# Tables of a state-space layer: the rotation table stays in SBUF, tiles share the operand ring, six table buffers, and the table build gets the last rank

## The chip, the cores and the metric

The kernel runs on one core of one Trainium2 chip. The metric is the device time of one execution in microseconds (us), as the median of several executions. Differences of under 0.3%, 8 us, are about what a measurement of this kernel cannot tell from no change.

## What is computed

Two layers on x, 1024 tokens by 1024 channels in float32. Layer 0 mixes tokens with RWKV-7, layer 1 with a diagonal complex state-space layer (S5) behind which stands a gated linear unit (GLU). A dense MLP with squared ReLU follows each mixer, and after each of the four sublayers comes `LayerNorm(alpha * x + f(x))`. The mixer of layer 1, cut:

```python
def s5_mix(x, a_re, a_im, log_dt, b_re, b_im, c_re, c_im, d_skip, w_glu):
    mag = exp(dt * lam_re)                       # 64 groups x 64 states
    abar = mag * (cos(dt * lam_im) + i sin(dt * lam_im))
    bbar = (abar - 1) / lam * b                  # per group: 64 states x 16 channels
    # state over 1024 tokens, per group: h[t] = abar * h[t-1] + bbar @ u[t]
    y = real(c @ h) + u * d_skip
    z = gelu(y) @ w_glu
    return z[..., :d] * sigmoid(z[..., d:])

def sq_relu_mlp(x, w1, w2):
    return square(relu(x @ w1)) @ w2
```

## The kernel before

**Layout.** Channels lie on partitions. The tokens go in two halves of 512, A (`hA`, split operands `oAh`, `oAl`) and B (`hB`, `oBh`, `oBl`); each half is eight tiles of 128 x 512. Large products are made of three matmuls on operands that are split into a high and a low part (`mm3`): `whi` by the high part of x, `whi` by the low one, `wlo` by the high one. The products go to PSUM tiles `d`.

**Weights.** `wload` brings one 128 x 512 weight tile: a load on SP's DMA queue into `wraw` (two buffers), a cast to `whi` on ScalarE (ACT), a subtraction that gives `wlo` on VectorE (DVE). `whi` and `wlo` have three buffers each. SP issues nearly all transfers of the program, in program order; an issue that must wait for a buffer or for its data holds all that stand behind it.

**Order.** A scheduler orders each engine's instructions by a simulated timeline and by a priority number, lower first. The main line counts from 200000; `with rank(n)` gives a block of code other numbers. Before, the tables have 99500 (`S5R`), the layer norms 99000, `s5(0)` 99300 and `s5(1)` 99400, so all of these go ahead of the MLPs' work when they are ready.

**The main line around the change.** MLP of layer 0 on half A (`ma`) begins; the RWKV's output projection `wo(1)` for half B follows, sixteen weight tiles `wraw<-in_wo_dram`; then the rest of `ma`. Beside these `s5_tables()` builds the tables. Then `s5(0)` on half A stands beside the MLP of layer 0 on half B (`mb`), and `s5(1)` on half B beside the GLU of half A.

**The tables.** `s5_tables()` first makes the powers of abar, `pw`, from small 128 x 32 tiles (traced as `q`, numbered). `turns()` raises the angle to the eighth power and then doubles up a table `R` of 64 rotations (cosine, sine) and a third plane with the decay `mag`; it writes `R` to DRAM as `tR`, eight writes of 390 KB. Then, for each of eight blocks `f`, DVE expands `ca` and `bp` (lines 1261 to 1268), TensorE multiplies and transposes them, and ACT writes a padded tile `kpad`, from which eight small DMAs make a Toeplitz table `tT`; `tB` and `tC` are written also. These go to DRAM.

**The SSM.** `s5(H, h)` handles a half in four pairs of blocks. `inputs(f2)` transposes two tiles of h (`pu1` to `u1`), regroups them (`pu2` to `ug`), loads the block's `rot` from `tR` and `tb` from `tB`, and multiplies (`pbu`). `states` rotates the result, runs a scan with the decay (`tensor_tensor_scan`, twice for each block) and rotates back into `hb`. `outputs(f2)` loads `tt` and `tcm`, accumulates `py` from the inputs and the states, copies it to `y1`, transposes (`pyt`), makes `yg` with the skip and the GELU, and stores it to `s_y`. `yload` reads `s_y` back and splits it for the GLU. `tb`, `tt` and `tcm` share the tag `tab` with four buffers of 512 KB; `u1` and `y1` share a tag with two. `optile(H)` hands out the next tile of the ring that holds the split operands of half H.

The decay scan reads the third plane of the loaded table, whose first column is zero for each of its four groups:

```python
V.tensor_tensor_scan(gf, rot[:, 2].rearrange("p g n -> p (g n)"), gf, 0.0, op0=ALU.mult, op1=ALU.add)
```

Of the kernel before, what the change touches and what calls it, by code (L numbers as in the profile page):

```python
# [29 lines left out]
S5R = 99500  # L30
# [3 lines left out]
JB = 4  # L34
LN8R = 400000
# [37 lines left out]
def trunk(ctx, tc, A):  # L73
# [1046 lines left out]
    tR = dr.tile([KT, 128, 3, 4, NSC + 1], F32, name="tR")  # L1120

    def turns(rp, mg, re, im, x, y):

        R = rp.tile([128, 3, 32, NSC + 1], F32, name="R")
        V.memset(R[:, :, :, 0], 0.0)
        for _ in range(SL.bit_length() - 1):
            V.tensor_mul(x, re, re)
            V.tensor_mul(y, im, im)
            V.tensor_mul(im, re, im)
            V.tensor_sub(re, x, y)  # L1130
            V.tensor_scalar(im, im, 2.0, None, op0=ALU.mult)
            V.tensor_mul(mg, mg, mg)
# [9 lines left out]
        V.tensor_copy(R[:, 0, :, 1], re)  # L1142
        V.tensor_copy(R[:, 1, :, 1], im)
        unit(R[:, 0, :, 1], R[:, 1, :, 1])
        S.copy(R[:, 2, :, 1:], mg.unsqueeze(2).broadcast_to([128, 32, NSC]))
        j = 1
        while j < NSC:
            sp_ = [128, 2, 32, j]
            w1, w2 = (rp.tile([128, 2, 32, NSC // 2], F32, tag=nm, name=nm, bufs=1)[:, :, :, 0:j] for nm in ("rx", "ry"))
            a, b = R[:, 0:2, :, 1 : j + 1], R[:, 0:2, :, j + 1 : 2 * j + 1]  # L1150
            V.tensor_mul(w1, a, R[:, 0:1, :, j : j + 1].broadcast_to(sp_))
            V.tensor_mul(w2, a, R[:, 1:2, :, j : j + 1].broadcast_to(sp_))
            V.tensor_sub(b[:, 0], w1[:, 0], w2[:, 1])
            V.tensor_add(b[:, 1], w1[:, 1], w2[:, 0])
            j *= 2
            unit(R[:, 0, :, j], R[:, 1, :, j])
        for f in range(KT):
            SP.dma_start(tR[f], R[:, :, 4 * f : 4 * f + 4])

    def s5_tables():  # L1160
# [40 lines left out]
        V.tensor_mul(pw[:, 1, :, 1], mg, tq)  # L1201
        for j in (1, 2, 4):

            sp_ = [128, 2, 32, j]
            w1, w2 = (pp.tile([128, 2, 32, 4], F32, tag=nm, name=nm, bufs=1)[:, :, :, 0:j] for nm in ("wx", "wy"))
# [26 lines left out]
        kpads = [pq.tile([128, 4, 16, 16], F32, name=f"kpad{j}") for j in range(2)]  # L1232
# [3 lines left out]
        bc = pq.tile([128, 2, 2, 32, 16], F32, name="bc")  # L1236
# [3 lines left out]
        bb, b2, c2 = (pq.tile([128, 2, 32, 16], F32, name=nm) for nm in ("bb", "b2", "c2"))  # L1240
# [7 lines left out]
        S.copy(b2[:, 1], bb[:, 0])  # L1248
        for ri in range(2):
            S.mul(c2[:, ri], bc[:, 1, 1 - ri], -1.0)  # L1250
        c1 = bc[:, 1]
        S.mul(c1[:, 1], c1[:, 1], -1.0)
        for f in range(KT):
# [3 lines left out]
            ca = pq.tile([128, 4, 2, 9, 16], F32, tag="ca", name="ca", bufs=1)  # L1257
            bp = pq.tile([128, 4, 2, 8, 16], F32, tag="bp", name="bp", bufs=1)

            def expand(dst, x, y, npow):  # L1260
                S.copy(dst[:, :, :, 0], x[:, :, gs].rearrange("p r g c -> p g r c"))
                w = pq.tile([128, 4, 2, 8, 16], F32, tag="tw", name="tw", bufs=1)[:, :, :, 0 : npow - 1]
# [27 lines left out]
            bs = pq.tile([128, 4, 2, 128], F32, tag="bs", name="bs", bufs=1)  # L1290
# [7 lines left out]
        late.close()  # L1298

    def s5(H, h):  # L1300
        ug, hs = [], []

        def inputs(f2):

            u1 = s5p.tile([128, 2, 8, 4, 16], F32, tag="u1", name="u1", bufs=2)
            for j in range(2):
# [4 lines left out]
                S.copy(u1[:, j].rearrange("p g s c -> p s g c"), p.rearrange("p s (g c) -> p s g c", g=8))  # L1311
            for j in range(2):
                f = 2 * f2 + j
                p = pc.tile([128, HT], F32, tag="c", name="pu2").rearrange("p (g n) -> p g n", g=8)
                for g in range(8):
                    for e in range(2):
                        PE.matmul(p[64 * (1 - e) : 64 * (1 - e) + 64, g], u1[:, j, g].rearrange("p s c -> p (s c)"),  # L1317
                                  sel[:, e], start=True, stop=True)
# [13 lines left out]
                states(f, p, rot)  # L1332

        def states(f, p, rot):
# [4 lines left out]
            def temps():  # L1339
                return [optile(H, l).bitcast(F32).rearrange("p (r g n) -> p r g n", r=2, g=4) for l in "hl"]  # L1340

            g = s5p.tile([128, 2, 4, NSC + 1], F32, tag="g", name="g", bufs=2)
            h_ = s5p.tile([128, 2, 4, NSC + 1], F32, tag="hb", name="hb", bufs=4)
            for t in (g, h_):
                if H == 0:
                    V.memset(t[:, :, :, 0], 0.0)
                else:
                    V.tensor_copy(t[:, :, :, 0], cy[:, :, 4 * f : 4 * f + 4])
            t1, t2 = temps()
# [7 lines left out]
            t1, t2 = temps()  # L1357
            V.tensor_mul(t1, g[:, :, :, 1:], cos)
            V.tensor_mul(t2, g[:, :, :, 1:], sin)
            V.tensor_sub(h_[:, 0, :, 1:], t1[:, 0], t2[:, 1])  # L1360
            V.tensor_add(h_[:, 1, :, 1:], t1[:, 1], t2[:, 0])
            if H == 0:
                V.tensor_copy(cy[:, :, 4 * f : 4 * f + 4], h_[:, :, :, NSC])
# [229 lines left out]
```

## Time and profile before

| | us |
|---|---|
| median of three executions | 2673.59 (2672.07 to 2679.01) |
| the profiled execution | 2674.25 |
| its span | 2672.5 |
| PE busy | 2495.2 (93%) |
| DVE busy | 1846.4 (69%) |
| ACT busy | 1133.2 (42%) |
| POOL busy | 629.8 (24%) |
| mean granted clock of TensorE | 0.96 |

The median is over three executions without a profile; the durations come from the profiled one, whose span runs from its first instruction to its last. PE is TensorE's matmuls, PEld its weight loads, DVE is VectorE, ACT is ScalarE, POOL is GpSimd, SP issues DMAs. A row of a wait reads: waiting engine, operation and line, the releaser, then total us, times, longest us. Matmuls are pipelined, so their busy time overlaps. A granted clock of 0.50 means that TensorE ran at half speed. In names such as `wraw_11913<-in_wo_dram` the number tells buffers apart, and the left side is written from the right one.

### The profile page before, as it was taken

Reading aid. Unit: us, or ns where it says so; the run is one execution under the profiler, and the core shown is the slowest. Engines: PE = TensorE matmul, PEld = TensorE weight load, DVE = VectorE, ACT = ScalarE, POOL = GpSimd, SP = SyncE. Lnnn points to the kernel's source line nnn. Section 1 sums busy time; section 2 is a strip of 40 time slices with the busy share of each in tenths; the row PEclk is TensorE's granted clock in tenths of the full one; section 3 lists DMA queues with packets and bytes.
Section 4 is the critical chain, followed back from the end, with each engine's and each line's share of the span. In section 5 each row is a group of like instructions: output and inputs, shape, how many; then the busy total and the mean of one; then the engine's idle time right before and its main releaser. Section 6 shows DMA issues by size and latency. Waiting matters only on the chain.

```text
span 2672.5 us, 43745 instructions
## 1 busy us (share of the span) xinstructions
PE 2495.2 (93%) x16624; PEld 2022.1 (76%) x16624; DVE 1846.4 (69%) x3271; ACT 1133.2 (42%) x2028; POOL 629.8 (24%) x532
## 2 busy tenths in 40 slices
PE   7899979989889999888899999998999999999996
PEld 5678757788667777766777888886777888888875
DVE  7367677487896868799785555775587656565576
ACT  7555665554444334245433333433453322323234
POOL 3121542342442222011100011200233313223111
PEclk9999889998889999999999999998999999999998
DMA  4765455663323324456465333264222111111133
GB/s 152 243 217 182 155 166 178 206 183 126 97 74 92 93 93 141 132 155 154 148 224 179 99 95 96 90 210 143 91 83 79 56 51 52 52 51 52 52 103 99
DMA packets 213074, 330.31 MB, mean 124 GB/s; under 512 B 20736, under 2 KB 85376, under 8 KB 212864
## 3 DMA queue, kind: packets, MB, share of 16 engines
q1 hardware_dynamic: 212864, 327.52, 39.3%
q8 instruction: 131, 2.15, 0.3%
q14 instruction: 79, 0.65, 0.1%
HBM read 260.28 MB, written 67.16 MB: 123 GB/s over the span
## 4 chain that ended last, share of the span: by engine, by line
PE 54%; DVE 11%; DMA 4%; issue 2%; ACT 1%; SPq 1%; POOL 1%; ACTq 0%; DVEq 0%; POOLq 0%
PE d L198 40%; PE d L1040 9%; DVE wlo L153 2%; DMA wraw<-in_mw_dram 2%; DMA yl<-s_y 1%; PE pu L1317 1%; DVE hA L1003 1%; PE pbu L1331 1%; DVE qbuf L153 0%; DVE hA L880 0%; ACT whi L152 0%; PE py L1383 0%; DMA s_y<-yg 0%; DVE tw L1267 0%; DVE ca L1266 0%
## 5 line engine op out<-in xcount | busy, mean ns | idle before, releaser
L152 ACT CAST whi<-wraw 128x512 fp32r<-128x512 f32 x524 | 324.3, 619 | 748.5 <-PE d L198 430.3
L153 DVE TENSOR_TENSOR wlo<-wraw,whi 128x512 fp32r<-128x512 f32 x524 | 409.1, 782 | 271.9 <-ACT whi L152 266.0
L198 PE MATMUL d<-qbuf,whi 128*128 128x512 f32 (+1 forms) x1344 | 414.5, 391 | 21.4 <-DVE hA L1003 13.7
L198 PE MATMUL d<-oAh,whi 128*128 128x512 f32 (+1 forms) x768 | 310.8, 412 | 14.2 <-ACT ev L428 9.3
L198 PE MATMUL d<-oAh,wlo 128*128 128x512 f32 (+1 forms) x768 | 309.4, 409 | 9.7 <-DVE wlo L153 6.3
L198 PE MATMUL d<-oAl,whi 128*128 128x512 f32 (+1 forms) x768 | 306.7, 403 | 8.2 <-DVE oAl L153 8.2
L198 PEld LDWEIGHTS d<-qbuf,whi 128*128 128x128 f32 x1344 | 248.5, 192 | 80.2 <-DVE hA L1003 15.8
L198 PE MATMUL d<-qbuf,wlo 128*128 128x512 f32 (+1 forms) x672 | 259.3, 388 | 6.5 <-DVE wlo L153 6.3
L987 POOL TENSOR_TENSOR rl<-rl 128x512 f32<-128x512 f32 x80 | 90.8, 1136 | 704.2 <-ACT rl L986 677.9
L198 PE MATMUL d<-oBh,whi 128*128 128x512 f32 x512 | 204.0, 400 | 13.5 <-ACT whi L152 10.4
L198 PE MATMUL d<-oBh,wlo 128*128 128x512 f32 x512 | 203.7, 399 | 8.1 <-DVE wlo L153 8.1
L198 PE MATMUL d<-oBl,whi 128*128 128x512 f32 x512 | 202.5, 396 | 0.0
L198 PEld LDWEIGHTS d<-oAh,whi 128*128 128x128 f32 (+1 forms) x768 | 147.3, 194 | 49.2 <-ACT ev L428 11.6
L198 PEld LDWEIGHTS d<-oAh,wlo 128*128 128x128 f32 (+1 forms) x768 | 147.2, 193 | 44.9 <-DVE wlo L153 8.5
L198 PEld LDWEIGHTS d<-oAl,whi 128*128 128x128 f32 (+1 forms) x768 | 147.8, 194 | 39.3 <-DVE oAl L153 10.1
L198 PEld LDWEIGHTS d<-qbuf,wlo 128*128 128x128 f32 x672 | 128.1, 191 | 35.0 <-DVE wlo L153 9.4
L198 PE MATMUL d<-qh,wlo 128*128 128x512 f32 x384 | 151.4, 394 | 0.0
L198 PE MATMUL d<-ql,whi 128*128 128x512 f32 x384 | 150.6, 392 | 0.0
L198 PE MATMUL d<-qh,whi 128*128 128x512 f32 x384 | 149.3, 389 | 0.0
L198 PEld LDWEIGHTS d<-oBh,whi 128*128 128x128 f32 x512 | 97.3, 191 | 37.8 <-ACT whi L152 12.4
L1003 DVE TENSOR_TENSOR hB<-hB,d 128x512 f32<-128x512 f32 (+1 forms) x168 | 104.4, 632 | 30.6 <-PE d L198 28.8
L198 PEld LDWEIGHTS d<-oBh,wlo 128*128 128x128 f32 x512 | 97.4, 190 | 31.7 <-DVE wlo L153 10.0
(455 smaller groups left out, 5175.1 us busy)
## 6 DMA issues: line engine op xcount, KB each, us to landing
wraw<-in_mw_dram SPq DMA_DIRECT2D x376, 256.0 KB, 2.7
wraw<-in_glu_dram SPq DMA_DIRECT2D x64, 256.0 KB, 2.7
low<-wlo SPq DMA_DIRECT2D x52, 256.0 KB, 2.8
wlo<-low SPq DMA_DIRECT2D x52, 256.0 KB, 3.8
raw<-in_mw_dram SPq DMA_DIRECT2D x48, 256.0 KB, 2.6
wraw<-in_wk_dram SPq DMA_DIRECT2D x32, 256.0 KB, 3.4
wraw<-in_wr_dram SPq DMA_DIRECT2D x32, 256.0 KB, 4.0
wraw<-in_wv_dram SPq DMA_DIRECT2D x32, 256.0 KB, 4.4
```

Source lines behind the costliest of these rows:

```text
L152: S.copy(hi, src)
L153: (e or V).tensor_sub(lo, src, hi.bitcast(F32))
L198: bulk.append((PE.matmul(p, w, x, **kw).ins, x.shape[-1]))
L987: G.tensor_mul(r, r, r)
L1003: V.tensor_add(z, z, p)
L1040: PE.matmul(p, w[:, k], x, start=not add and k + j == 0, stop=k == 3 and j == 2, skip_group_check=True)
L1317: PE.matmul(p[64 * (1 - e) : 64 * (1 - e) + 64, g], u1[:, j, g].rearrange("p s c -> p (s c)"), sel[:, e], start=True, stop=True)
L1331: PE.matmul(p[qs, ri, g2], tb[:, g2, ri, qs], u[:, 2 * g2 + par], start=True, stop=True)
```

## The change

- The rank of the table build goes from 99500 to 300000, behind all of the main line.
- `R` keeps two planes of 64 rotations, and lives with `mag` in a pool of its own in SBUF until `s5(1)` is done. The eight `tR` writes and the sixteen `rot` loads are gone. `states` reads `R` in place, and makes the decay tile `mg` [128, 4, 65] itself: a memset of the first column on DVE and a broadcast copy on ACT.
- The last doubling step of the turns (32 rotations) goes in two chunks of 16, so that its scratch fits the tiles `bb` and `b2`. All of the table's tiles now lie in one pool, `pp`; `bc` no longer takes the place of `R`. `c2` takes the place of B's raw values in `bc`.
- `u1`, the temporaries of `states` and the states `h_` take tiles of the operand ring (`optile(H)`); the tag `hb` is gone. `y1` has its own tag with one buffer.
- `tab` has six buffers rather than four (`TABB`).
- The carry `cy` is computed from the temporaries by two small operations for each block, in place of one copy.

```diff
-S5R = 99500
+S5R = 300000
+TABB = 6
...
-    tR = dr.tile([KT, 128, 3, 4, NSC + 1], F32, name="tR")
-
-    def turns(rp, mg, re, im, x, y):
-
-        R = rp.tile([128, 3, 32, NSC + 1], F32, name="R")
-        V.memset(R[:, :, :, 0], 0.0)
+    def turns(R, mag, re, im, x, y, w):
...
-        S.copy(R[:, 2, :, 1:], mg.unsqueeze(2).broadcast_to([128, 32, NSC]))
         j = 1
         while j < NSC:
-            sp_ = [128, 2, 32, j]
-            w1, w2 = (rp.tile([128, 2, 32, NSC // 2], F32, tag=nm, name=nm, bufs=1)[:, :, :, 0:j] for nm in ("rx", "ry"))
-            a, b = R[:, 0:2, :, 1 : j + 1], R[:, 0:2, :, j + 1 : 2 * j + 1]
...
+            for c in range(0, j, 16):
+                n = min(j, 16)
+                sp_ = [128, 2, 32, n]
+                w1, w2 = (t[:, :, :, 0:n] for t in w)
+                a, b = R[:, :, :, c : c + n], R[:, :, :, j + c : j + c + n]
...
-        for f in range(KT):
-            SP.dma_start(tR[f], R[:, :, 4 * f : 4 * f + 4])
...
-        with tc.tile_pool(name="rp", bufs=1) as rp:
-            turns(rp, mg, tr, tq, sn, cs)
-        late = ExitStack()
-        pq = late.enter_context(tc.tile_pool(name="pq", bufs=1))
+        V.tensor_copy(mag, mg)
+        turns(R, mag, tr, tq, sn, cs, (bb, b2))
...
-            u1 = s5p.tile([128, 2, 8, 4, 16], F32, tag="u1", name="u1", bufs=2)
+            u1 = [temp(l).rearrange("p (g s c) -> p g s c", g=8, s=4) for l in "hl"]
...
-                rot = s5p.tile([128, 3, 4, NSC + 1], F32, tag="rot", name="rot", bufs=2)
-                SP.dma_start(rot, tR[f])
-                tb = s5p.tile([128, 4, 2, 128], F32, tag="tab", name="tb", bufs=4)
+                tb = s5p.tile([128, 4, 2, 128], F32, tag="tab", name="tb", bufs=TABB)
...
-            cos, sin = (rot[:, k, :, 1:].unsqueeze(1).broadcast_to(sh) for k in range(2))
+            cos, sin = (R[:, k, gs].unsqueeze(1).broadcast_to(sh) for k in range(2))
...
-            h_ = s5p.tile([128, 2, 4, NSC + 1], F32, tag="hb", name="hb", bufs=4)
+            mg = s5p.tile([128, 4, NSC + 1], F32, tag="mg", name="mg", bufs=2)
+            V.memset(mg[:, :, 0], 0.0)
+            S.copy(mg[:, :, 1:], mag[:, gs].unsqueeze(2).broadcast_to([128, 4, NSC]))
+            t1, t2, h_ = (temp(l).rearrange("p (r g n) -> p r g n", r=2, g=4) for l in ("hlh", "hll")[f % 2])
...
-                V.tensor_tensor_scan(gf, rot[:, 2].rearrange("p g n -> p (g n)"), gf, 0.0, op0=ALU.mult, op1=ALU.add)
-            t1, t2 = temps()
+                V.tensor_tensor_scan(gf, mg.rearrange("p g n -> p (g n)"), gf, 0.0, op0=ALU.mult, op1=ALU.add)
...
-                V.tensor_copy(cy[:, :, 4 * f : 4 * f + 4], h_[:, :, :, NSC])
+                V.tensor_sub(cy[:, 0, gs], t1[:, 0, :, n], t2[:, 1, :, n])
+                V.tensor_add(cy[:, 1, gs], t1[:, 1, :, n], t2[:, 0, :, n])
...
-            y1 = s5p.tile([128, SL, 4, 2, 16], F32, tag="u1", name="y1", bufs=2)
+            y1 = s5p.tile([128, SL, 4, 2, 16], F32, tag="y1", name="y1", bufs=1)
```

The order of the instructions differs in two regions: from the first table arithmetic (1040 us before) to the end of `s5(0)`, and in `s5(1)`. Three places follow. Line numbers after the change are a few lines off those of before: the weight load of line 173 is that of line 174, the sum of line 1003 that of 1004.

SP around the weight loads of `wo(1)`, before: loads into `wraw` (`in_mw_dram` are the MLP's weights), the writes of `tR`, the loads of the raw matrices `bc`, and the first table written, `tC` of one block.

```order
L958 DMA yl<-s_y 128x512
L173 DMA wraw<-in_mw_dram 128x512 x7
L173 DMA wraw<-in_wo_dram 128x512 x12
L1158 DMA tR<-R 384x1x260 x8
L173 DMA wraw<-in_wo_dram 128x512 x2
L1239 DMA bc<-in_s5bc_dram 128x512 x4
L173 DMA wraw<-in_wo_dram 128x512 x2
L173 DMA wraw<-in_mw_dram 128x512 x2
L1272 DMA tC<-ca 1024x1x128
L173 DMA wraw<-in_mw_dram 128x512 x2
```

The same place after:

```order
L959 DMA yl<-s_y 128x512
L1235 DMA bc<-in_s5bc_dram 128x512 x2
L174 DMA wraw<-in_mw_dram 128x512
L1235 DMA bc<-in_s5bc_dram 128x512 x2
L959 DMA yl<-s_y 128x512
L174 DMA wraw<-in_mw_dram 128x512
L959 DMA yl<-s_y 128x512
L174 DMA wraw<-in_mw_dram 128x512 x7
L174 DMA wraw<-in_wo_dram 128x512 x16
L174 DMA wraw<-in_mw_dram 128x512 x5
L1267 DMA tC<-ca 1024x1x128
L174 DMA wraw<-in_mw_dram 128x512 x4
```

The eight writes are gone, the four `bc` loads stand ahead of the last loads `yl` for `wo(1)`, the sixteen weight loads stand in one run, and the first `tC` comes three weight loads later.

DVE at the first sum of the MLP of half A (`hA_7515`) that stands among the table arithmetic, before. `q4`, `q6` to `q9` are the table's small tiles, `wx` and `wy` its scratch, `oBl` a split operand of `wo(1)`:

```order
L1131 TENSOR_SCALAR q8_12752<-q8_12752 128x32
L1132 TENSOR_TENSOR q4_12748<-q4_12748 128x32
L1207 TENSOR_TENSOR wx_12787<-pw_12744 128x64x2
L1208 TENSOR_TENSOR wy_12788<-pw_12744 128x64x2
L1127 TENSOR_TENSOR q6_12750<-q9_12753 128x32
L1128 TENSOR_TENSOR q7_12751<-q8_12752 128x32
L1132 TENSOR_TENSOR q4_12748<-q4_12748 128x32
L1209 TENSOR_TENSOR pw_12744<-wx_12787,wy_12788 128x32x2
L1210 TENSOR_TENSOR pw_12744<-wx_12787,wy_12788 128x32x2
L153 TENSOR_TENSOR oBl_11691<-yl_11688,oBh_11690 128x512
L1129 TENSOR_TENSOR q8_12752<-q9_12753,q8_12752 128x32
L1003 TENSOR_TENSOR hA_7515<-hA_7515,d_11410 128x512
```

The sum of the same place after (`hA_7514`), with the rows ahead of it:

```order
L1171 TENSOR_SCALAR q2_12750<-q2_12750 128x32
L1172 TENSOR_TENSOR q4_12752<-q1_12749,q2_12750 128x32
L1209 COPY mag_12744<-q4_12752 128x32
L1130 TENSOR_TENSOR mag_12744<-mag_12744 128x32
L154 TENSOR_TENSOR oBl_11690<-yl_11687,oBh_11689 128x512
L1130 TENSOR_TENSOR mag_12744<-mag_12744 128x32
L1174 TENSOR_TENSOR q5_12753<-q1_12749,q3_12751 128x32
L1004 TENSOR_TENSOR hA_7514<-hA_7514,d_11409 128x512
L154 TENSOR_TENSOR wlo_11450<-wraw_11447,whi_11449 128x512
L1130 TENSOR_TENSOR mag_12744<-mag_12744 128x32
L1177 TENSOR_SCALAR q8_12756<-q5_12753 128x32
L1004 TENSOR_TENSOR hA_7554<-hA_7554,d_11417 128x512
```

The powers `pw` are no longer ahead of it; a part of the small operations on `q` and `mag` is.

SP in `s5(1)`, before: table loads `tt`, `tcm`, stores of `yg` to `s_y`, loads `yl` of it, and weight loads of the GLU.

```order
L1406 DMA s_y_131<-yg_17780 128x512
L1372 DMA tt_17931<-tT_137 128x1024
L1406 DMA s_y_131<-yg_17793 128x512
L173 DMA wraw_18952<-in_glu_dram 128x512
L1374 DMA tcm_17933<-tC_139 128x1024
L173 DMA wraw_18986<-in_glu_dram 128x512
L1372 DMA tt_18014<-tT_137 128x1024
L1374 DMA tcm_18016<-tC_139 128x1024
L958 DMA yl_18748<-s_y_131 128x512
L958 DMA yl_18754<-s_y_131 128x512
L1372 DMA tt_18018<-tT_137 128x1024
L1374 DMA tcm_18020<-tC_139 128x1024
```

The same place after (`tt_17902` is the `tt_17931` of before, `yg_17752` its `yg_17780`):

```order
L1368 DMA tcm_17900<-tC_139 128x1024
L1366 DMA tt_17902<-tT_137 128x1024
L1368 DMA tcm_17904<-tC_139 128x1024
L174 DMA wraw_18637<-in_glu_dram 128x512
L174 DMA wraw_18670<-in_glu_dram 128x512
L1400 DMA s_y_131<-yg_17752 128x512
L1400 DMA s_y_131<-yg_17765 128x512
L1366 DMA tt_17985<-tT_137 128x1024
L174 DMA wraw_18676<-in_glu_dram 128x512
L1368 DMA tcm_17987<-tC_139 128x1024
L1366 DMA tt_17989<-tT_137 128x1024
L1368 DMA tcm_17991<-tC_139 128x1024
```

Before, the two stores stand among the four loads of the third pair; after, all four come ahead of the stores. The four loads of the last pair follow the stores in both, without the two `yl` loads that stand between them before.

More of the change, by code (lines that the diff above doesn't have):

```diff
@@ L1201, in s5_tables @@
         V.tensor_mul(pw[:, 1, :, 1], mg, tq)
+        bb, b2 = (pp.tile([128, 2, 32, 16], F32, name=nm) for nm in ("bb", "b2"))
         for j in (1, 2, 4):
             sp_ = [128, 2, 32, j]
-            w1, w2 = (pp.tile([128, 2, 32, 4], F32, tag=nm, name=nm, bufs=1)[:, :, :, 0:j] for nm in ("wx", "wy"))
+            w1, w2 = (t[:, :, :, 0:j] for t in (bb, b2))
             x, y = pw[:, :, :, 1 : j + 1], pw[:, :, :, j + 1 : 2 * j + 1]
@@ L1230, in s5_tables @@
         V.tensor_mul(ci, ci, den)
-        kpads = [pq.tile([128, 4, 16, 16], F32, name=f"kpad{j}") for j in range(2)]
+        kpads = [pp.tile([128, 4, 16, 16], F32, name=f"kpad{j}") for j in range(2)]
         for kpad in kpads:
             G.memset(kpad[:, :, 0:8], 0.0)
-        bc = pq.tile([128, 2, 2, 32, 16], F32, name="bc")
+        bc = pp.tile([128, 2, 2, 32, 16], F32, name="bc")
         for j in range(2):
@@ L1288, in s5_tables @@
                     SP.dma_start(tv[par, g2], bass.AP(src.tensor, src.offset, [src.ap[0], (16, SL), src.ap[1]]))
-            bs = pq.tile([128, 4, 2, 128], F32, tag="bs", name="bs", bufs=1)
+            bs = pp.tile([128, 4, 2, 128], F32, tag="bs", name="bs", bufs=1)
             for hf in range(2):
@@ L1297, in s5_tables, with temp @@
             SP.dma_start(tB[f], bs)
-        late.close()
     def s5(H, h):
         ug, hs = [], []
+        def temp(l):
+            return optile(H, l).bitcast(F32)
         def inputs(f2):
-            u1 = s5p.tile([128, 2, 8, 4, 16], F32, tag="u1", name="u1", bufs=2)
+            u1 = [temp(l).rearrange("p (g s c) -> p g s c", g=8, s=4) for l in "hl"]
             for j in range(2):
@@ L1437, in trunk @@
     run(ma)
+    sctx = ctx.enter_context(ExitStack())
+    rp = sctx.enter_context(tc.tile_pool(name="rp", bufs=1))
+    R = rp.tile([128, 2, 32, NSC], F32, name="R")
+    mag = rp.tile([128, 32], F32, name="mag")
     with tc.tile_pool(name="pp", bufs=1) as pp:
```

55 lines of the change are left out of this document (26 added, 29 removed).

## Prediction

> **What bounds the kernel now.** I read the page first, then the stretch in which the tables are built and used, cut into stages. The first two parts of the page, cut to the engines that matter:
>
> ```profile
> span 2672.5 us, 43745 instructions
> PE 2495.2 (93%) x16624; PEld 2022.1 (76%) x16624; DVE 1846.4 (69%) x3271; ACT 1133.2 (42%) x2028; POOL 629.8 (24%) x532
> ...
> PE   7899979989889999888899999998999999999996
> ...
> DVE  7367677487896868799785555775587656565576
> ...
> PEclk9999889998889999999999999998999999999998
> ```
>
> TensorE is the bound, so its dips under 9 are what there is to win. One slice is 2672.5 / 40 = 66.8 us. Slices 17 to 20 (8888, from 1069 us) are the table build, with DVE at 8 and 7 to begin with; slice 28 (from 1804 us, the PEclk 8 in a run of nines) is the SSM of half B. Outside of the stages below the order of the two programs is the same, so I leave those 2139 us at their old time. The stretch in windows (columns: length; busy us and count of PE, PEld, DVE, ACT, POOL; granted PE clock; DMA share; GB/s). I call the rows A to E:
>
> ```profile
> 1040.00:1094.00 54.00, 50.22 (x209) 40.31 (x208) 47.34 (x147) 22.54 (x39) 4.25 (x4) 0.94 0.49 157
> 1094.00:1150.00 56.00, 46.32 (x193) 37.24 (x192) 41.55 (x73) 13.25 (x23) 4.39 (x4) 0.91 0.52 150
> 1150.00:1311.00 161.00, 137.60 (x782) 106.08 (x781) 137.96 (x207) 73.85 (x137) 30.43 (x22) 0.96 0.60 156
> 1311.00:1443.00 132.00, 126.15 (x1329) 102.41 (x1328) 102.18 (x190) 50.60 (x88) 7.71 (x7) 0.99 0.62 207
> 1740.00:1870.00 130.00, 119.13 (x1270) 95.58 (x1270) 89.39 (x156) 41.74 (x73) 7.37 (x8) 0.95 0.53 179
> ```
>
> A is the first wave of table arithmetic beside MLP A, B the projection `wo(1)`, C the table expansions beside MLP A, D the SSM of half A, E the SSM of half B. What can be won in a stage is PE's idle time, plus the length times what the clock lacks of 1 (a stage at 0.94 loses 6%): A 3.8 + 3.2 = 7.0, B 9.7 + 5.0 = 14.7, C 23.4 + 6.4 = 29.8, D 5.9 + 1.3 = 7.2, E 10.9 + 6.5 = 17.4; together 76 us.
>
> The clock's share comes in stretches that stand behind idle time of PE:
>
> ```profile
> 1060.70:1067.50 6.80, 5.90 (x14) 4.63 (x15) 6.80 (x21) 4.25 (x7) 0.00 (x0) 0.50 0.26 85
> 1129.00:1139.20 10.20, 4.37 (x10) 3.46 (x11) 2.34 (x3) 1.67 (x3) 1.00 (x2) 0.50 0.88 233
> 1835.50:1845.70 10.20, 8.79 (x100) 7.77 (x100) 1.84 (x2) 1.38 (x3) 0.00 (x0) 0.50 0.23 87
> ```
>
> Half clock for 6.8 or 10.2 us costs 3.4 or 5.1 us of the work that lies in it, so a wait costs its own length and about as much again. What PE waited for, stage by stage (total, times, longest; A, B, then C, D, E):
>
> ```profile
> PE d L198 <- DVE hA L1003: 3.8, 2, 3.6
> ...
> PE d L198 <- ACT whi L152: 7.9, 1, 7.9
> ...
> PE d L198 <- DVE wlo L153: 8.6, 5, 3.6
> PE d L198 <- DVE hA L1003: 6.0, 5, 3.0
> ...
> PE pyt L1401 <- DVE yg L1403: 2.8, 1, 2.8
> PE py L1391 <- DMA tcm<-tC: 2.1, 1, 2.1
> ...
> PE py L1391 <- DMA tcm<-tC: 3.6, 1, 3.6
> PE d L198 <- ACT oBh L152: 3.1, 2, 2.6
> PE py L1383 <- DMA tt<-tT: 2.8, 1, 2.8
> ```
>
> Each stage is held by something else: A and C by DVE that comes late with MLP sums and weight splits, B by one weight tile that is late, D and E by table loads.
>
> **The change, stage by stage.**
>
> *A, rank of the tables.* The wait of 3.6 us on `hA` is a sum of the MLP that DVE does behind table arithmetic: in the order before, the row of `hA_7515` comes behind some twenty table rows, and in the order after, the sum of the same place comes ahead of nearly all of them. A's 12.23 us of DVE work on the table's small tiles `q` (69 instructions; columns length, DVE busy, clock, DMA) moves behind the MLP's:
>
> ```profile
> 1040.00:1094.00 54.00, 12.23 (x69) 0.94 0.49 157
> ```
>
> The 3.6 us and its 3.4 us of half clock should go. I take 6 of A's 7.0.
>
> *B, the copy of the rotation table.* SP issues in order. Its row in B (start, length, then operation; the third and fifth are weight loads of `wo(1)`), and what one of its later issues waited for:
>
> ```profile
> 1085.16 32.57 SPq L173 DMA_DIRECT2D wraw<-in_wo_dram  x12
> 1118.66 8.14 SPq L1158 DMA_DIRECT2D tR<-R  x8
> 1126.89 2.08 SPq L173 DMA_DIRECT2D wraw<-in_wo_dram  x2
> 1133.65 1.75 SPq L1239 DMA_DIRECT2D bc<-in_s5bc_dram  x4
> 1135.53 0.98 SPq L173 DMA_DIRECT2D wraw<-in_wo_dram  x2
> ...
> SPq L1239 <- DMA tR<-R: 4.5, 1, 4.5
> ```
>
> The thirteenth weight load is issued behind 8.14 us of `tR` writes, and the fifteenth behind the `bc` loads, which wait 4.5 us for the writes since their buffer takes the place of `R`. PE's 7.9 us on `whi` is this, and so is half clock over 10.2 us (10.2 - 4.37 of it PE does nothing at all). After the change there are no writes, `bc` has a place of its own, and the sixteen loads stand in one run on SP. 7.9 goes, and of the clock's 5.0 some 4 goes: 12. The rest of B's idle time, 9.7 - 7.9 = 1.8, I keep.
>
> *C, the expansions.* Here DVE is busy 137.96 of 161 us, and takes over the 12.23 us that left A (the turns that stand in B have gaps of PE to lie in). I make it 138 + 12 = 150 us of DVE work. The expansions themselves are unchanged (columns behind the bar: us in all, mean ns; idle time ahead):
>
> ```profile
> L1266 DVE TENSOR_TENSOR ca<-pw,bc 128x512 f32<-128x512 f32 x16 | 12.3, 800 | 0.0
> L1267 DVE TENSOR_TENSOR tw<-pw,c 128x512 f32<-128x512 f32 x16 | 11.0, 726 | 0.1
> L1268 DVE TENSOR_TENSOR ca<-ca,tw 128x1024 f32<-128x1024 f32 x8 | 10.6, 1320 | 0.0
> L1267 DVE TENSOR_TENSOR tw<-pw,b 128x448 f32<-128x448 f32 x16 | 10.5, 696 | 0.0
> L1266 DVE TENSOR_TENSOR bp<-pw,bb 128x448 f32<-128x448 f32 x16 | 10.3, 681 | 0.0
> L1268 DVE TENSOR_TENSOR bp<-bp,tw 128x896 f32<-128x896 f32 x8 | 10.3, 1282 | 0.1
> ```
>
> So C can't become shorter than about 150 + some waits of DVE. What the rank turns around is the order: `hA` sums (6.0 us of PE's waits) and `wlo` splits (8.6) come ahead of expansions. The other side is SP. The 64 writes of `tT`, in groups of 8, still stand among the weight loads, and SP waits there for a padded tile that ACT writes from DVE's result:
>
> ```profile
> SPq L1288 <- ACT kpad L1283: 25.5, 8, 5.1
> ```
>
> 25.5 / 8 = 3.2 us a group. With the tables last this wait can grow. PE has what is already loaded: two raw and three split tiles. Ends: all 29.8 gained, or 7 lost (first rival). I take 6, the `hA` waits, since those are what the new order moves most plainly.
>
> *D, loads for half A.* The 16 `rot` loads go (390 KB each, for both halves) and `tab` has six places rather than four, so table loads may run further ahead. 2.1 us on `tcm` goes; I take 2. The order of the rest of D is the old one.
>
> *E, loads for half B.* The waits of 3.6 and 2.8 us, and half clock over the 10.2 us behind them (5.1 us): 11.5. In the order before, one `tcm` load stands behind two stores of `s_y` and a weight load; in the order after, four table loads run ahead of those stores. The 3.1 on `oBh` is the end of the chain through `s_y` and stays. I take 11 of 17.4.
>
> *What is added.* Sixteen copies of the decay into [128, 4, 65] tiles, on ACT. The nearest row is a copy of its size, 369 ns; 16 make 6 us on an engine that is 42% busy. Their source is ready long before, so a copy can only delay the scan that it feeds. On DVE: 16 memsets, 8 more carries, and four operations more in the turns. The nearest rows:
>
> ```profile
> L717 ACT COPY o<-pR 128x256 f32<-128x256 f32 x32 | 11.8, 369 | 6.4 <-PE pR L715 6.1
> ...
> L1363 DVE COPY cy<-hb 128x8 f32<-128x8 f32 x8 | 1.3, 163 | 0.0
> L1346 DVE MEMSET g<- 128x8 f32 x6 | 0.4, 65 | 0.0
> ```
>
> 16 x 0.065 + 8 x 0.163 = 2.3 us, and for four turns at most 163 ns apart from their elements, 0.7: 3 us over D and E and the build. DVE is busy 102 of 132 and 89 of 130 us there, so the end inside the sum is 0 and the other 3. I take 0. `u1`, the temporaries and `h_` now take tiles from the ring that also holds the split operands of the half; a state tile then lives from its making to its `py` products. Nothing in the trace shows this ring short, since before it held only temporaries; ends are 0 and one wait like D's 2.8 on `yg` for each half, 5.6. `y1` has one place of its own where it shared two with `u1`; its next copy waits for the transposes of the pair before, and the next pair's `py` products stand between: the same ends. I take 0 for both, because the order of PE shows no later `py`.
>
> Sum: 6 + 12 + 6 + 2 + 11 = 37 us. The profiled execution took 2674.25 us (span 2672.5), 0.7 above the median of the runs: 2674.25 - 37 = 2637.
>
> **The skill against the trace.** The half-clock stretches here are 6.8 and 10.2 us, and stand behind waits of 3.6, 7.9, and of 3.6 and 2.8 in E. The Trainium skill, page "TensorE: Matmul & The Clock Gate", Part 1, says that the clock is either whole or half, falls after about one idle window (some 3.4 us) and wants as long a busy one to return. The trace agrees on the two values and on the multiples of 3.4; by that rule E's second wait, 2.8, would not have halved anything alone, and closing only the first would return the clock. By the rule the estimate for E would stay 11 if both waits go.
>
> A rule against the change: the Trainium skill, page "Perfetto Trace Analysis", section on the per-instruction lifecycle, says that VectorE and ScalarE lose a fixed time on each instruction to a read-write bubble, so the ratio is worst for small operands. The 8-element copy's 163 ns agrees. By it the 44 added small operations would be priced by their count, not their elements; at 163 ns each 7 us of engine time rather than the 3 and 6 above, which changes nothing while they lie beside PE's work.
>
> **Rivals.**
>
> *DVE is the bound in C.* For it: 137.96 busy of 161, and 12.23 more to come. If DVE's waits in C for the weight casts stay as they are,
>
> ```profile
> DVE wlo L153 <- ACT whi L152: 18.0, 11, 4.9
> ```
>
> C needs 138 + 12 + 18 = 168 us, 7 more than now, and D gets none of its 2. Against: a DVE that is behind doesn't wait for casts. 6 + 12 + 11 - 7 = 22: 2652.
>
> *SP is blocked by the tables' writes: slower.* Each group of `tT` writes holds the next weight loads until its `kpad` is there. A block's expansions take DVE 65.0 / 8 = 8.1 us (the six groups above). If SP arrives a whole block early, each group costs 8.1, less the 12 matmuls of a tile that is already split (by C's row 137.60 / 782 = 0.176 us each, 2.1), so 6.0; eight make 48. Against 6 + 12 + 2 + 11 = 31 gained outside C: 2674 + 17 = 2691. It decides from 31 / 8 = 3.9 us a group. Against it: before, 3.2 us a group cost PE no wait named so.
>
> *E's loads aren't what the order says.* E's gain needs that loads leave SP earlier; SP may be held there by stores all the same. Then 6 + 12 + 6 = 24: 2650.
>
> *C is won whole.* The order lets PE run through C: 37 + 24 = 61: 2613. Against: DVE at 150.
>
> *Nothing to speak of.* New waits take what old ones leave, as the fillers of PE are the same matmuls either way: 2674.
>
> **How the numbers follow.** The sum as it stands has 0.38 (own range 2624 to 2649, half of C's gain or of E's either way); DVE as the bound 0.20; E's loads 0.20; C whole 0.07; blocked SP 0.08; nothing 0.07. Faster by over 0.3% (8 us, about what a measurement of this kernel can tell from no change) are the first four less the tails that come near 2666: 0.82. Within: 0.09. Slower: 0.09. The range runs from the case of C whole to beyond DVE as the bound, 2612 to 2668; outside lie the blocked SP, most of "nothing" and a little of the low end.
>
> **What would show it.** Right: no `tR` write on SP, PE without a wait over 2 us in B and its clock there near 1; the waits on `tcm` and `tt` gone from E and its clock over 0.98; `hA` no longer a releaser of PE in A. Wrong: C longer than 161 us, or SP's wait for `kpad` over 60 us; a line of PE waiting over 5 us for a table tile (`ca`, `bp`) or for a ring tile; E with waits of the same size on `yg` or `oBh`. What would make the sum wrong is above all C, where I gave 6 of 29.8 to an engine that gets more work.

## The result and the profile after

The changed kernel takes 2633.18 us in the median of four executions (2625.45 to 2638.96), the one before 2672.83 (2669.59 to 2679.01). The ratio is 0.9844, with a 95% interval from 0.9828 to 0.9861. The forecast was 2637, with a range from 2612 to 2668. The profiled execution took 2631.33 us, 42.9 less than that of before.

The head of its page. Column 17 of the PE row, an 8 before, is a 9 now, and so are the three behind it:

```profile
span 2629.6 us, 43742 instructions
PE 2477.9 (94%) x16624; PEld 2006.3 (76%) x16624; DVE 1849.6 (70%) x3299; ACT 1134.8 (43%) x2043; POOL 638.5 (24%) x532
...
PE   7899979988989999999999999999989999999997
...
DVE  7367777586897777899895555777687656556576
...
PEclk9998979999889999999999999999999999999998
```

TensorE runs the same 16624 matmuls in both, and outside of the two regions in the same order. So a place in the program can be named by its number in PE's order: the first matmul that starts behind 1040 us of before starts at 1042.48 after. In the same way I carried over the borders of the stages A to E (inside a region the order differs, so the borders between A, B and C are by count alone):

```profile
1042.48:1094.55 52.07, 48.47 (x210) 38.31 (x208) 42.40 (x119) 20.98 (x39) 7.59 (x6) 1.00 0.57 183
1094.55:1138.27 43.72, 43.72 (x192) 35.87 (x191) 42.41 (x98) 10.74 (x19) 3.46 (x2) 1.00 0.30 97
1138.27:1283.69 145.42, 137.15 (x782) 104.63 (x781) 138.48 (x204) 72.65 (x137) 33.92 (x22) 0.99 0.56 143
1283.69:1414.98 131.29, 123.44 (x1329) 99.97 (x1328) 103.72 (x216) 56.22 (x102) 7.76 (x7) 0.99 0.64 219
1711.95:1829.06 117.11, 112.42 (x1271) 91.60 (x1270) 88.88 (x166) 43.82 (x81) 7.84 (x8) 0.99 0.50 169
```

| stage | before | after | won | forecast |
|---|---|---|---|---|
| A | 54.0 | 52.1 | 1.9 | 6 |
| B, `wo(1)` | 56.0 | 43.7 | 12.3 | 12 |
| C, expansions | 161.0 | 145.4 | 15.6 | 6 |
| D, SSM of half A | 132.0 | 131.3 | 0.7 | 2 |
| E, SSM of half B | 130.0 | 117.1 | 12.9 | 11 |
| sum | 533.0 | 489.6 | 43.4 | 37 |

PE has no idle time in B at all (43.72 of 43.72 us). On SP the sixteen loads stand in one run, as the order said (start, length, operation):

```profile
1084.91 43.77 SPq L174 DMA_DIRECT2D wraw<-in_wo_dram  x16
1130.11 13.21 SPq L174 DMA_DIRECT2D wraw<-in_mw_dram  x5
1144.12 0.59 SPq L1267 DMA_DIRECT2D tC<-ca  x1
```

What is left of PE's waits, of A, C, D and E (B has none):

```profile
PE d L199 <- DVE hA L1004: 2.5, 4, 1.1
...
PE d L199 <- DVE hA L1004: 4.0, 4, 1.6
PE pk L1274 <- DVE ca L1263: 2.0, 3, 1.2
...
PE pyt L1395 <- DVE yg L1397: 2.6, 1, 2.6
...
PE py L1377 <- DMA tt<-tT: 2.4, 1, 2.4
PE pu L1306 <- DVE oBl L1344: 1.3, 1, 1.3
PE d L199 <- DVE wlo L154: 0.9, 1, 0.9
```

The 8.6 us on `wlo` in C and the 7.9 on `whi` in B are gone. In E, one wait on a table is left, `tt` with 2.4 us; that on `tcm` and that on `oBh` are gone. In A, `hA` still makes PE wait, four times, so two of the signs that I named for a right forecast did not come in full; none of the signs for a wrong one came.

### The profile page after: what moved, and what is told of

Read it like the earlier page. It is cut to its first block, busy times and chain, and to the rows that moved or that the text cites. A ratio compares the mean times of both kernels' runs of the same rounds, so it can differ in the third digit from the quotient of the medians.

```text
span 2629.6 us, 43742 instructions
## 1 busy us (share of the span) xinstructions
PE 2477.9 (94%) x16624; PEld 2006.3 (76%) x16624; DVE 1849.6 (70%) x3299; ACT 1134.8 (43%) x2043; POOL 638.5 (24%) x532
## 4 chain that ended last, share of the span: by engine, by line
PE 55%; DVE 9%; issue 4%; DMA 2%; ACT 2%; POOL 1%; SPq 0%; ACTq 0%; DVEq 0%; POOLq 0%
PE d L199 42%; PE d L1041 9%; DVE wlo L154 2%; DMA wraw<-in_mw_dram 1%; ACT whi L153 1%; DVE hA L1004 1%; ACT hA L905 0%; POOL rl L988 0%; DVE qbuf L154 0%; DVE hB L904 0%; PE pu L1313 0%; PE pbu L1325 0%; PE py L1377 0%; DVE hA L881 0%; DVE oAl L154 0%
## 5 line engine op out<-in xcount | busy, mean ns | idle before, releaser
L199 PE MATMUL d<-oAh,whi 128*128 128x512 f32 (+1 forms) x768 | 310.1, 412 | 13.2 <-ACT ev L429 8.5
L988 POOL TENSOR_TENSOR rl<-rl 128x512 f32<-128x512 f32 x80 | 96.7, 1209 | 693.0 <-ACT rl L987 688.0
L1004 DVE TENSOR_TENSOR hA<-hA,d 128x512 f32<-128x512 f32 x144 | 97.5, 683 | 26.7 <-PE d L199 25.3
```

Source lines behind the costliest of these rows:

```text
L199: bulk.append((PE.matmul(p, w, x, **kw).ins, x.shape[-1]))
L988: G.tensor_mul(r, r, r)
L1004: V.tensor_add(z, z, p)
```

## The experiments

For these, two stretches are compared whose ends lie where all orders agree: the first from 1040 to 1500 us of before (tables and SSM of half A), the second from 1740 to 2000 (SSM of half B). Between them the stretch from 1500 to 1740 took 240.01 or 240.02 us in every kernel. The part ahead of 1040, where all kernels have the same order, took anything from 1035.0 to 1052.4 us in the profiled executions; that is the scatter of whole executions, and why the stretches tell more than the totals. Rows are of the windows view: the ends of the stretch, its length, and then the columns as above.

**The change once more** (`e14_again`), for the scatter of a stretch.

> The changed kernel once more, with the same order of instructions, for the scatter of a stretch from one execution to the next. From 1040 to 1500 us of before it took 429.5 us, from 1740 to 2000 it took 246.9: within 4 and 3 us of that, if differences of 10 us and more between versions are to mean anything.

2632.60 us, ratio 0.9849 (0.9829 to 0.9869). Second stretch, before, after, and again:

```profile
1740.04:2000.10 260.06, 239.26 (x1785) 192.38 (x1784) 179.32 (x278) 106.15 (x183) 47.00 (x39) 0.96 0.40 133
...
1711.95:1958.81 246.86, 230.60 (x1784) 186.47 (x1783) 182.51 (x289) 107.66 (x189) 48.94 (x39) 0.99 0.39 126
...
1705.77:1956.68 250.91, 236.16 (x1785) 190.62 (x1783) 182.84 (x289) 107.61 (x189) 48.36 (x39) 0.96 0.37 124
```

The first stretch came out within 0.4 us (429.85), the second 4.0 apart, one more than expected; the clock is what differs (0.99 and 0.96). Differences under 4 us in one stretch say nothing below.

**The rank put back** (`e1_rank_old`), all else as changed.

```diff
-S5R = 300000
+S5R = 99500
```

> The changed kernel with the tables' rank put back to 99500; everything else as changed (no rotation table in DRAM, six table buffers, tiles in the ring). Theory (the rank gives the gain of the build stages A and C, B's gain needs only that the writes of tR are off SP): A's 2 and most of C's 15 us are lost again, B's 12 and E's 13 stay: about 2632 + 15 = 2647 us; the wait of the weight split for its cast in C grows from 3.8 back towards 18 us. Rival (C gained because SP has fewer transfers to issue, not because of the rank): within 5 us of 2632.

**The rank alone** (`e2_rank_only`), in the kernel of before.

```diff
-S5R = 99500
+S5R = 300000
```

> The kernel of before with one edit, the tables' rank 300000. In its order the writes of tR stand behind the sixteen weight loads of wo(1), not among them. Theory: A's 2, B's 12 and C's 15 us come, E's 13 do not: 2673 - 29 = 2644 us, and PE waits for tt and tcm in E as before (6 us, a half clock behind them). Rival (B and C need tR gone from SP): 2673 - 5 = 2668 us or more.

2641.01 us, 0.9877 (0.9844 to 0.9911), with the rank put back; 2658.48, 0.9946 (0.9926 to 0.9966), with the rank alone. First stretch before, after, without the new rank, and with it alone:

```profile
1040.04:1500.03 459.99, 417.27 (x2758) 332.81 (x2757) 358.34 (x659) 179.43 (x320) 53.07 (x43) 0.96 0.55 163
...
1042.48:1471.93 429.45, 409.74 (x2757) 325.53 (x2756) 356.43 (x677) 179.73 (x329) 59.02 (x43) 0.99 0.53 161
...
1035.71:1472.58 436.87, 410.21 (x2757) 328.18 (x2756) 356.23 (x677) 181.18 (x329) 58.10 (x43) 0.98 0.52 158
...
1042.86:1490.92 448.06, 418.03 (x2757) 326.40 (x2756) 358.08 (x659) 179.78 (x319) 60.20 (x43) 0.98 0.56 168
```

Of the 30.5 us that the change wins here, the rank alone brings 11.9, all but the rank 23.1. The theory that the rank gives the gain of A and C is too simple: without it only 7.4 is lost, not 17. A loses nothing (51.8 us). B and C, which I take together since the order inside them differs, took 217.0 us before and 189.1 after the change, 196.9 without the rank and 208.6 with it alone. Of the theory's signs, the wait of the weight split for its cast in C did come back, 14.0 us without the rank. With the rank alone PE also still waits 2.8 us in B, for a weight that is loaded among the writes of `tR`: on SP two of these stand ahead of the sixteenth load, and seven ahead of the weight that follows it. The median of 2658 lies between the two expectations for that run, 2644 and 2668. In the second stretch the rank alone brings 2.8, as expected next to nothing, and without the rank E keeps its gain (244.8).

**`bc` in a place of its own** (`e8_bc_own`), on top of the rank alone.

```diff
-        bc = pq.tile([128, 2, 2, 32, 16], F32, name="bc")
+        bc = pp.tile([128, 2, 2, 32, 16], F32, name="bc")
```

> The kernel of before with the rank 300000 and one more edit: bc has a place of its own and does not take that of R, so its loads no longer wait for the writes of tR. The rank alone won 12 us between 1040 and 1500 us of before where the whole change won 30. Theory (the table expansions, which need bc, stood behind the tR writes' landing, and after that in the way of the MLP): most of the missing 18 comes, 12 or more: 2658 - 12 = 2646 us or less. Rival (tR and its writes themselves cost it): under 5 us, 2653 to 2658.

2651.60 us, 0.9905 (0.9871 to 0.9939); 441.3 in the first stretch. That is 6.8 better than the rank alone, between the theory's 12 and the rival's 5. DVE's timeline shows what is still missing. Before, and then in this version (start, length; in brackets the idle time ahead and what ended it):

```profile
1126.94 0.69 DVE L971 SCALAR_TENSOR_TENSOR hB<-hB,d 128x512 f32<-128x512 f32 x1 [4.03 <-PE d L198]
...
1134.81 1.34 DVE L153 TENSOR_TENSOR wlo<-wraw,whi 128x512 fp32r<-128x512 f32 x2 [6.45 <-ACT whi L152]
1138.20 1.23 DVE L1243 TENSOR_TENSOR b<-bc,q 128x1024 f32<-128x1024 f32 x1 [2.06 <-DMA bc<-in_s5bc_dram]
```

```profile
1132.90 0.69 DVE L153 TENSOR_TENSOR wlo<-wraw,whi 128x512 fp32r<-128x512 f32 x1 [5.59 <-ACT whi L152]
1133.64 1.23 DVE L1243 TENSOR_TENSOR b<-bc,q 128x1024 f32<-128x1024 f32 x1
```

Before, DVE's first row of the expansion work (line 1243) starts when `bc` has landed, and SP could issue the loads of `bc` only at 1133.65, right behind the landing of the last `tR` write at 1133.46. In the second version `bc` is there in time, but `bb`, `b2` and the other tiles of the pool `pq` still lie where `R` was. The same row starts at 1133.64, and the last write landed at 1133.35. What ended the idle time ahead of it is by the trace the cast of a weight, whose load was issued among the writes; that the place of these tiles also held DVE there fits the times and the code, and is not shown.

**The `tR` writes put back**, with the new rank (`e4_tr_writes`) and with the old one (`e12_tr_old_rank`). In both the table's tiles keep places of their own, so nothing waits for the writes.

```diff
+        for f in range(KT):
+            SP.dma_start(tR[f], R[:, :, 4 * f : 4 * f + 4])
```

> The changed kernel, which also writes its rotation table to DRAM (eight writes of 256 KB; nothing reads them; 8.1 us of SP before, when they were 390 KB). With the last rank they stand behind the weight loads of wo(1). Theory (a write costs only where it stands ahead of weight loads that PE is about to need): at most 3 us more, 2632 to 2635. Rival (SP's issue time is paid wherever it stands): the whole 8 us, with a half clock as in B before, 12: 2644.

> The changed kernel with the tables' rank put back to 99500, which also writes its rotation table to DRAM (eight writes of 256 KB that nothing reads). In its order the writes stand behind the thirteenth weight load of wo(1), as in before; bc does not wait for them. With the old rank and no writes, PE's work from 1040 to 1500 us of before took 436.9 us. Theory (the writes ahead of needed weight loads starve PE in B): PE waits 4 us or more for whi or wlo in wo(1) with a half clock behind it, and the stretch takes 443 to 449 us. Rival (before, the stall was made by bc that waited for the writes, 4.5 us, not by the writes' 8.1): within 3 us of 437.

With the new rank 2631.93 us, 0.9839 (0.9820 to 0.9858), and 432.1 in the first stretch: 2.6 more, inside the scatter. With the old rank 2646.10, 0.9902 (0.9884 to 0.9919), and 440.8, 4.0 more than without the writes (436.9): between the two theories, and no more than two executions of one kernel lay apart. SP has the writes among the loads of `wo(1)` again, and PE hardly notices:

```profile
1119.97 6.76 SPq L1158 DMA_DIRECT2D tR<-R  x8
1126.83 1.04 SPq L174 DMA_DIRECT2D wraw<-in_wo_dram  x2
...
PE d L199 <- ACT whi L153: 1.0, 1, 1.0
```

What DVE waited for, about B: with the old rank and the writes, after, and in the version with `bc` alone moved:

```profile
DVE wlo L154 <- ACT whi L153: 2.7, 3, 1.0
```

```profile
DVE wlo L154 <- ACT whi L153: 0.7, 2, 0.5
```

```profile
DVE wlo L153 <- ACT whi L152: 8.8, 3, 5.6
```

So here 6.8 us of writes ahead of weight loads cost PE 1.0. For the 7.9 of before, ACT and PE show when it ended:

```profile
1134.15 1.27 ACT L152 CAST whi<-wraw 128x512 fp32r<-128x512 f32 x2 [13.29 <-DMA wraw<-in_wo_dram]
1134.83 0.80 PE L198 MATMUL d<-oBh,whi 128*128 128x512 f32 x1 [7.92 <-ACT whi L152]
```

The cast is that of the thirteenth and fourteenth weight tile. SP issued their loads right behind the writes, at 1126.89 and 1128.04, and they landed after 7.2 and 6.7 us, where the four loads ahead of the writes took 2.6 or 2.7. The `bc` loads were issued at 1133.65 and the last two weight loads at 1135.53, too late to have a part in this wait. So the rival, that `bc` made the stall, is refuted by the trace of before. It was the writes, by their 8.1 us on SP and by the late landing of the loads behind them. In the run here the two loads behind the writes landed after 3.5 and 3.6 us. It differs from before in two things at once: the writes are of 256 KB, not of 390, and thirteen weight tiles were loaded ahead of them, not twelve (the expectation took thirteen for both). Their shares aren't separated.

**Table buffers**: four (`e3_tab4`) and five (`e13_tab5`).

```diff
-TABB = 6
+TABB = 4
```

> The changed kernel with four table buffers rather than six. Theory (E's loads run ahead because of the two more buffers): E loses about 11 of its 13 us, D next to nothing: 2632 + 11 = 2643 us, with waits of PE for tt or tcm over 5 us in E. Rival (the rot loads that no longer stand on SP gave E's gain): E keeps it, 2632 us within 4.

> The changed kernel with five table buffers. From 1740 to 2000 us of before six took 246.9 us and four 259.7. Theory (E's gain needs a whole next pair of tables, four tiles, beside the two in use, so six): nearer to four buffers, 253 to 260 us. Rival (any buffer more lets the loads leave ahead of the stores): 247 to 250.

Four: 2638.72 us, 0.9878 (0.9854 to 0.9901). Five: 2637.62, 0.9870 (0.9837 to 0.9902). Second stretch, with four and with five:

```profile
1706.78:1966.47 259.69, 238.17 (x1785) 188.86 (x1784) 182.68 (x289) 108.28 (x189) 47.80 (x39) 0.96 0.37 124
...
1712.33:1961.51 249.18, 233.08 (x1785) 186.24 (x1784) 181.97 (x287) 106.89 (x189) 47.97 (x39) 0.99 0.38 127
```

With four, all of E's gain is gone, though no `rot` load is left. With five it is there: the fifth buffer decides, not a whole pair, and the theory behind the second of these runs was wrong. The waits with four are not those that I expected:

```profile
PE d L199 <- DVE wlo L154: 10.8, 6, 3.7
PE d L199 <- DVE oBl L154: 4.3, 2, 4.0
PE pm L879 <- DVE yg L1397: 2.7, 1, 2.7
```

No table tile is in it. The last table load is issued 86.2 us into the stretch, with six buffers 70.7, and the last load of `yl` lands at 116.0 rather than at 104.6. So the whole chain of the SSM ends later, and PE waits at its end, for `oBl` and `yg`, with 13.7 us of half clock at that place. In the first stretch four buffers lost nothing (425.4). All the kernels here bear it out: the second stretch took 255.8 to 261.5 us in the six executions with four buffers, that of before included, 249.2 with five, and 244.8 to 251.5 in the seven with six.

**The `rot` loads put back** (`e5_rot_loads`), to be read against the run with four buffers.

```diff
+                rot = s5p.tile([128, 2, 4, NSC], F32, tag="rot", name="rot", bufs=2)
+                SP.dma_start(rot, tR[f])
```

> The changed kernel with four table buffers, which writes the rotations to DRAM and loads them block by block again (256 KB each, two planes; the decay tile as changed). To be read against the run with four table buffers (2638.72). Theory (rot loads cost only where a table load queues behind them): D and E together lose 0 to 4 us, 2639 to 2643. Rival (a rot load holds SP until a buffer is free, 12.8 and 12.2 us of SP's waits in D and E before, and that is paid): 10 us more, 2649.

2643.21 us, 0.9873 (0.9843 to 0.9904). 430.4 and 261.5, against 425.4 and 259.7 without: 6.8 in sum, between the two expectations and near the scatter. In E they cost 1.8, inside the scatter. Nor was their room needed for the buffers that give E's gain. By the sizes of its tiles, the pool of the SSM takes 44.1 KB of each partition after the change, and just as much with `rot` and five table buffers in it, and five were enough. Before, the pool took 52.3 KB, and the 16.1 KB in which `R` and `mag` now lie were free at that time. With a fifth table buffer (4 KB) it would have taken 56.3, against the 60.2 of pool, `R` and `mag` after the change. So the kernel of before had room for five; it was not run with them.

**The states out of the ring** (`e9_hb_own`), with four table buffers.

```diff
-            t1, t2, h_ = (temp(l)... for l in ("hlh", "hll")[f % 2])
+            t1, t2 = (temp(l)... for l in "hl")
+            h_ = s5p.tile([128, 2, 4, NSC], F32, tag="hb", name="hb", bufs=4)
```

> The changed kernel with four table buffers and the states h_ in buffers of their own again (four), so that the operand ring holds only u1 and the temporaries. To be read against four table buffers with the states in the ring: 425.4 us from 1040 to 1500, 259.7 from 1740 to 2000. Theory (the ring is never short, the move costs nothing in itself): both within 3 us. Rival (a state that sits in the ring delays the split operands of the GLU): 4 us or more faster in one of the two stretches.

2639.94 us, 0.9879 (0.9856 to 0.9903); 428.3 and 257.6 against 425.4 and 259.7. Both are within 3 us, as expected: the ring costs nothing that can be seen.

**Two tries to go on.** Both took up what seemed to hold C: SP's waits for `kpad`, and DVE. `e6_tt_on_act` issues the `tT` writes from ACT, `e10_tw_pool` gives half of the products `tw` to POOL.

```diff
-                    SP.dma_start(tv[par, g2], ...)
+                    S.dma_start(tv[par, g2], ...)
```

```diff
-                    V.tensor_mul(w[:, :, ri], pi_, ...)
+                    (G if ri else V).tensor_mul(w[:, :, ri], pi_, ...)
```

> The changed kernel with the 64 writes of tT issued by ACT, right behind the copy into kpad that they wait for, and not by SP. SP's wait for kpad in C (14.9 us in 5) goes. Theory (C is now bound by DVE, busy 138.48 of 145.42 us): little comes of it, 2628 to 2633, and ACT's issues may cost some of that. Rival (SP's waits hold the weight loads): C shortens by 8 us or so, 2624.

> The changed kernel with half of the products tw of the expansions (16 of 32, some 11 us on DVE) on POOL. Theory (C is bound by DVE): C shortens by most of the 11, total 2622 to 2626. Rival (the expansions' own chain, or POOL's squares of the MLP behind them, decide): no gain or a loss, 2632 to 2640.

Neither is faster: 2641.50 us, 0.9870 (0.9836 to 0.9903), with 436.7 in the first stretch, and 2642.43, 0.9870 (0.9840 to 0.9900), with 433.7; the change has 429.5. So taking the waits for `kpad` off SP wins nothing; why their move costs 7 us is open. With POOL, DVE's rows in the first stretch, after and in this version, tell why:

```profile
L154 DVE TENSOR_TENSOR wlo<-wraw,whi 128x512 fp32r<-128x512 f32 x118 | 85.8, 730 | 36.1 <-ACT whi L153 36.1
L1262 DVE TENSOR_TENSOR tw<-pw,bc 128x512 f32<-128x512 f32 x16 | 11.2, 737 | 0.0
```

```profile
L154 DVE TENSOR_TENSOR wlo<-wraw,whi 128x512 fp32r<-128x512 f32 x118 | 91.1, 773 | 30.0 <-ACT whi L153 30.0
L1262 POOL TENSOR_TENSOR tw<-pw,bc 128x512 f32<-128x512 f32 x8 | 13.0, 1624 | 43.8 <-ACT bc L1246 23.7 <-DVE bp L1263 20.1
L1262 DVE TENSOR_TENSOR tw<-pw,bc 128x512 f32<-128x512 f32 x8 | 7.3, 910 | 0.0
```

Sixteen operations left DVE, and its busy time rose from 356.43 to 359.81 us: those that stayed take longer, the same `tw` 910 ns rather than 737. The Trainium skill, page "Perfetto Trace Analysis", section "Optimizing Scalar/DVE Operations", says that VectorE and GpSimd share a read port of SBUF, so that moving work from one to the other may not help. These rows agree.

No version of these beats the change by more than its scatter.

## Why the prediction was right, step by step

The sum was 37 and the median moved by 39.7 (42.9 between the profiles). It is right in E and as a whole; in B the size is right by two errors that cancel, C was sized too low and A too high. So the total also owes something to luck.

- **C, 6 forecast, 15.6 measured.** The size of this term failed twice. I took 6 for PE's waits on `hA`, and of these only 2.0 went (6.0, now 4.0); the waits on `wlo`, for which I took nothing, went whole, 8.6 us, and those on `whi`, `rl` and `pk` fell too. PE's idle time in C fell from 23.4 to 8.3 us. I held the gain down because of "takes over the 12.23 us that left A ... 138 + 12 = 150 us of DVE work", and that did not happen. DVE's work on the tiles `q`, B before, and then A and B after the change (length, DVE busy, clock, DMA):

```profile
1094.00:1150.00 56.00, 7.56 (x26) 0.91 0.52 150
...
1042.48:1094.55 52.07, 10.56 (x49) 1.00 0.57 183
1094.55:1138.27 43.72, 10.85 (x44) 1.00 0.30 97
```

Of the 12.23 us, 10.56 stayed in A. What left A was above all work on `R` (8.04 us there, now 1.84), and it went to B (13.75, now 21.58), not to C, where DVE's busy time stayed (137.96, now 138.48). B had the room: before, DVE stood idle there for 4.03 + 6.45 + 2.06 us, as the rows above show. I had counted B's stall as PE's alone. Over A to C, DVE is busy 226.9 of 271.0 us before (84%) and 223.3 of 241.2 after (93%). So DVE is near its limit there, as the first rival said. But its 168 us did not come: most of the 12.23 stayed in A, and DVE's waits for casts in C fell from 18.0 to 3.8. That DVE is the bound is not shown: the one try to relieve it did not shorten its busy time.

- **B, 12 and 12.3.** I took 7.9 of idle time and 4 of the clock, and kept 1.8 of idle time. All 9.7 of idle time went, also the 1.8, a wait on `wlo` that DVE split behind expansions; the clock gave 2.6 (PE's busy time 46.3, now 43.7), since PE stood idle for much of the half clock. The cause is right for the thirteenth weight load behind the `tR` writes; that the fifteenth behind `bc` had a part in the 7.9 is wrong, as shown above. Either edit takes most of it away: 2.8 us of waits on `whi` are left with the rank alone, 1.0 with tiles of their own, the old rank and the smaller writes.
- **A, 6 and 1.9.** The half clock is gone (0.94 to 1.00), the idle time isn't: 3.8 us, 3.6 of it in one wait, became 3.6 in several, the longest 1.1. Nor does the gain need the rank, as I had it: A takes 51.8 us with the rank put back and 51.6 with the rank alone.
- **E, 11 and 12.9** (its longer stretch 13.2, in a second execution 9.2). The buffers carry it, as I said, and five are enough; that the wait on `oBh` would stay was wrong, since an earlier start moves the end of the chain too. The rival that the loads leave no earlier is refuted with six and with five buffers, and is true with four.
- **D, 2 and 0.7**, too little to tell.
- **The added work at 0.** The sixteen copies of the decay take 404 ns each rather than 369, and one wait of 0.4 us, of a weight load of TensorE, names them. That a copy "can only delay the scan that it feeds" is not so: ACT stood idle for 35.4 us in front of these copies, until a scan (line 1349) was done, and held what stood behind them.

```profile
L1336 ACT COPY mg<-mag x16: 397/404/407, 1297.2 to 1766.1; 128x256 f32<-128x256 f32 x16
```

- **SP blocked by `tT`.** SP's wait for `kpad` in C fell from 25.5 to 14.9 us, and taking it off SP didn't help.

Not settled: of the first stretch's 30.5 us, the rank, the place of `bc` and the rest (11.8 from there to the whole change) are each shown, but the rest holds the places of `bb`, `b2`, `ca` and the others together with the writes and the ring; with the writes put back, at 256 KB, 9.2 of the 11.8 remain (432.1), so the writes alone are not what counts most. Giving `pq` a place of its own in the kernel of before wasn't tried, nor five table buffers there.

## What to carry to other kernels

When two engines are both near their limit, look for the time in which the second one is idle although its next work is long known, and ask what that work waits for; here it was in part the memory of a tile that was still being written out, which no wait of the bound engine names (moving `bc` out of it won 6.8 us). A load that is issued behind large writes can be late twice, by their issue and by its own landing, 7.2 us rather than 2.7. A further buffer may be worth more than the transfers that are saved: the sixteen `rot` loads cost little, and the fifth table buffer was worth some 10 us. Add up the tiles before a layout is changed for its sake, since the room may be there. Compare stretches between places where two orders agree, since the total also holds the scatter of parts that the change does not touch.

## What the runs showed of the hardware

The clock halves behind shorter idle time than I took. After the change, a stretch of half clock begins right behind 1.57 us of idle time:

```profile
1159.54 1.18 PE L199 MATMUL d<-qbuf,whi 128*128 128x512 f32 x2 [1.57 <-DVE hA L1004]
...
1159.60:1163.00 3.40, 3.40 (x11) 2.74 (x11) 3.40 (x6) 1.85 (x4) 0.00 (x0) 0.50 0.78 104
```

while 2.64 us at 1390 us and 2.39 at 1788 bring 3.4 us of it each, and the 1.49 at 1359 none. The length of the idle time doesn't decide alone: before, 3.60 us that ended at 1212.7 brought none, and E's 10.2 us of half clock began at 1835.5, inside the wait of 2.8. What decides is open. By the rule of the Trainium skill, page "TensorE: Matmul & The Clock Gate", Part 1, an idle window of some 3.4 us is needed; the length of a stretch agrees, the threshold doesn't. And the first 1040 us, whose order is the same in all kernels here, differ by up to 17 us between the profiled executions, more than most of the edits are worth.
